# Rotating 96 images by 180 degrees: the last load cut by rows instead of columns, and the first store released by a copy

## The chip, the cores and the metric

The kernel runs on one core of one Trainium2 chip. The metric is the device time of one execution in microseconds (us): 121.89 us is the median of 3 runs before the change (121.85 to 122.08).

## What is computed

The input `x` holds 32 x 3 images of 256 x 256 numbers in float32, 25.17 MB. The reference turns each image by 180 degrees:

```python
def reference(x):
    return np.rot90(x, k=2, axes=(-2, -1)).astype(np.float32)
```

An image read as one line of 65,536 numbers is thus written in reverse order. There is no arithmetic: every byte is read once and written once.

## The kernel before

The 96 images are three groups of 32. In a group, each image is cut into 4 quarters of E = 16,384 numbers (64 KB), which makes 128 rows: row 4n + s is quarter s of image n. A row is one partition of an on-chip tile. The tiles `A`, `Bt` and `Ct` hold the three groups, one each, and all three fit on the chip at once. So a group's work is: load (8.39 MB), reverse each row inside its partition, store.

*Reversal.* `turn` does it in place by the vector engine (DVE), in 4 swaps of J = 2,048 columns from both ends. `swap` makes three copies, all on line 44: the reversed right piece goes to the spare tile `T`, the reversed left piece goes to the right place, and `T` goes to the left place. So a group needs 12 copies. In the profile they are named by tiles: `T<-Bt`, `Bt<-Bt`, `Bt<-T` are the three copies of one swap of group 1. `keep_in_program_order` keeps the copies in the order in which they are written. The order of the four quarters of an image is reversed by the store, which writes quarters with step -1 on the side of the memory (line 50).

*Queues.* Loads and stores are issued by SyncE (SP, the queue `q1`), except the load of `Bt`, which ScalarE issues (queue `q10`). A queue issues in program order, and an instruction whose wait isn't over holds everything behind it on that engine. Behind the queues are 16 DMA engines, which share each transfer by rows; one row, or the part of it that the transfer takes, is one packet. A transfer has a semaphore which is complete when all its rows have landed. A small memset of `Bt` (line 67) precedes the load of `Bt`, and so sets when that load is issued.

*Order.* The loads are issued one after the other at the start: `A`; `Bt` on the other queue; and `Ct` in three transfers (lines 69 to 71):

```python
    rows(2, 0, 0, E)
    ahead = rows(2, 1, 0, E - LAST)
    rows(2, 1, E - LAST, E)
```

They are the 64 even rows; the first 10,624 columns of the 64 odd rows (42,496 B of each row); and their last `LAST` = 5,760 columns (23,040 B of each). Then come the turn of `A`, the store of `A`, the turn and the store of `Bt`, and those of `Ct`.

The store of `A` needs the 12 copies of `A`. A dependence written by hand makes it wait for `ahead` as well, that is, until of all loads only the last columns of the odd rows are under way (lines 80 to 85). The store of `A` is the first on SP after the loads, so the other stores stand behind it.

Of the kernel before, what the change touches and what calls it, by code (L numbers as in the profile page):

```python
# [2 lines left out]

os.environ.setdefault("NEURON_RT_ULTRASERVER_MODE", "4")

# [4 lines left out]


@with_exitstack
def kernel(
    ctx: ExitStack,
    tc: tile.TileContext,
    x: bass.AP,
    out: bass.AP,
):
    nc = tc.nc  # L20
    P = 128

    B, C, H, W = x.shape
    L = H * W
    G = 32
    E = L // 4
    J = E // 8

    x4 = x.rearrange("b c h w -> (b c) (h w)").rearrange(
        "(g n) (s e) -> g (n s) e", n=G, s=4)  # L30
    o4 = out.rearrange("b c h w -> (b c) (h w)").rearrange(
        "(g n) (s e) -> g n s e", n=G, s=4)

    pool = ctx.enter_context(tc.tile_pool(name="slots", bufs=1))
    A = pool.tile([P, E], x.dtype, tag="A")
    Bt = pool.tile([P, E], x.dtype, tag="B")
    Ct = pool.tile([P, E], x.dtype, tag="C")
    T = pool.tile([P, J], x.dtype, tag="T")

    def back(t, lo, hi):  # L40
        return t[:, hi - 1:(lo - 1 if lo else None):-1]

    def copy(dst, src):
        tc.keep_in_program_order(nc.vector.tensor_copy(out=dst, in_=src))  # L44

    def load(t, g, lo, hi, queue=nc.sync):
        return queue.dma_start(out=t[:, lo:hi], in_=x4[g][:, lo:hi])

    def store(t, g, lo, hi):
        return nc.sync.dma_start(  # L50
            out=o4[g][:, ::-1, lo:hi], in_=t[:, lo:hi])

    def swap(t, lo, w):
        hi = E - lo - w
        copy(T[:, 0:w], back(t, hi, hi + w))
        copy(t[:, hi:hi + w], back(t, lo, lo + w))
        copy(t[:, lo:lo + w], T[:, 0:w])

    half = E // 2
    LAST = 5760  # L60

    def rows(g, first, lo, hi):
        return nc.sync.dma_start(
            out=Ct[first::2, lo:hi], in_=x4[g][first::2, lo:hi])

    load(A, 0, 0, E)
    nc.vector.memset(Bt[:, 0:256], 0.0)  # L67
    load(Bt, 1, 0, E, nc.scalar)
    rows(2, 0, 0, E)
    ahead = rows(2, 1, 0, E - LAST)  # L70
    rows(2, 1, E - LAST, E)

    def turn(t, lo, hi):
        while lo < hi:
            w = min(J, hi - lo)
            swap(t, lo, w)
            lo += w

    turn(A, 0, half)
    first = store(A, 0, 0, E)  # L80
    tc.add_manual_dep(
        first.ins, ahead.ins.name,
        mybir.DependencyInfo(
            mybir.DependencyClass.Sync, mybir.DependencyReason.DATA),
        reason="the first store waits for the loads' last columns but a few")
    turn(Bt, 0, half)
    store(Bt, 1, 0, E)
    turn(Ct, 0, half)
    store(Ct, 2, 0, E)


# [1 line left out]
_INS = ['x']  # L93
_OUTS = [((32, 3, 256, 256), 'float32')]


# [23 lines left out]
```

## Time and profile before

| | before |
|---|---|
| median of 3 runs | 121.89 us (121.85 to 122.08) |
| the profiled execution's own time | 122.06 us |
| its span | 120.3 us |
| DVE busy | 44.4 us, 37 instructions |
| a copy of 128 x 2,048 | 1.23 us |
| read and written | 25.17 MB and 25.17 MB, 418 GB/s over the span |
| packets of DMA | 960, 816 of them on q1 |
| first store (`A`) issued | 58.02 us |
| last store (`Ct`) issued | 84.97 us |

The span is the part of the execution from the program's first to its last instruction; the rest lies around it. The page of the profile divides the span into 40 slices of 3 us and shows for each how busy an engine was. An issue's time to landing goes from the instruction that issues the transfer to the completion of its semaphore, so it includes the time in the queue behind earlier transfers. Start times in the timeline are counted from the start of the span.

### The profile page before, as it was taken

To read this page: it belongs to the slowest core of one execution; us is meant where nothing else is said; L and a number is where in the kernel's file an instruction comes from. 1 tells how busy PE (TensorE), PEld (TensorE's weight loads), DVE (VectorE), ACT (ScalarE), POOL (GpSimd) and SP (SyncE) were. 2 spreads that over 40 slices of the span, in tenths; PEclk is the share of its full clock that TensorE was granted. 3 is DMA by queue.
4 is the path that set the end of the run, shared out by engine and by line. 5 is a ranking of instruction groups with operands and counts; after the bars stand their busy time and mean duration, and the time that the engine had idled before them with its cause. 6 is when DMAs were issued, how large, how long until landed. Compare 5 with 4: busy or idle time off the path is not lost.

```text
span 120.3 us, 96 instructions
## 1 busy us (share of the span) xinstructions
DVE 44.4 (37%) x37; POOL 0.2 (0%) x4
## 2 busy tenths in 40 slices
DVE  0000000000000899999999999999200000000000
POOL 0000000000000000000000000000000000000000
DMA  9888988898889988997999889988998899889980
GB/s 349 349 349 371 676 349 349 371 654 371 349 349 654 392 349 349 547 410 327 452 574 480 349 349 545 501 349 349 545 501 349 349 458 589 349 349 436 588 371 0
DMA packets 960, 50.33 MB, mean 418 GB/s; under 512 B 128, under 2 KB 128, under 8 KB 128
## 3 DMA queue, kind: packets, MB, share of 16 engines
q1 hardware_dynamic: 816, 41.94, 81.1%
q10 hardware_dynamic: 144, 8.39, 16.1%
HBM read 25.17 MB, written 25.17 MB: 418 GB/s over the span
## 4 chain that ended last, share of the span: by engine, by line
DVE 37%; DMA 32%; issue 1%
DMA A<-in_x_dram 32%; DVE T L44 12%; DVE A L44 8%; DVE Bt L44 8%; DVE Ct L44 8%
## 5 line engine op out<-in xcount | busy, mean ns | idle before, releaser
L44 DVE COPY T<-A 128x2048 f32<-128x2048 f32 x4 | 4.9, 1226 | 38.6 <-DMA A<-in_x_dram 38.5
L44 DVE COPY A<-A 128x2048 f32<-128x2048 f32 x4 | 4.9, 1227 | 0.1
L44 DVE COPY A<-T 128x2048 f32<-128x2048 f32 x4 | 4.9, 1227 | 0.1
L44 DVE COPY T<-Bt 128x2048 f32<-128x2048 f32 x4 | 4.9, 1227 | 0.1
L44 DVE COPY Bt<-T 128x2048 f32<-128x2048 f32 x4 | 4.9, 1227 | 0.1
L44 DVE COPY T<-Ct 128x2048 f32<-128x2048 f32 x4 | 4.9, 1227 | 0.1
L44 DVE COPY Ct<-T 128x2048 f32<-128x2048 f32 x4 | 4.9, 1227 | 0.1
L44 DVE COPY Bt<-Bt 128x2048 f32<-128x2048 f32 x4 | 4.9, 1226 | 0.1
L44 DVE COPY Ct<-Ct 128x2048 f32<-128x2048 f32 x4 | 4.9, 1226 | 0.1
L67 DVE MEMSET Bt<- 128x256 f32 x1 | 0.3, 272 | 0.9 <-PEq L104 0.9
L104 POOL MEMSET const-bfloat16-1.0<- 128x1 bf16 x1 | 0.1, 101 | 0.0
L104 POOL MEMSET const-uint8-127<- 128x1 uint8 x1 | 0.1, 101 | 0.0
L104 POOL MEMSET const-float32-0.0<- 128x1 f32 x1 | 0.1, 98 | 0.2 <-issue 0.2
L104 POOL MEMSET const-float32-1.0<- 128x1 f32 x1 | 0.1, 98 | 0.0
## 6 DMA issues: line engine op xcount, KB each, us to landing
Ct<-in_x_dram SPq DMA_DIRECT2D x1, 2656.0 KB, 56.2
Ct<-in_x_dram SPq DMA_DIRECT2D x1, 1440.0 KB, 59.1
A<-in_x_dram SPq DMA_DIRECT2D x1, 38.8
Ct<-in_x_dram SPq DMA_DIRECT2D x1, 50.5
Bt<-in_x_dram ACTq DMA_DIRECT2D x1, 43.2
out_dram<-A SPq DMA_DIRECT2D x1, 22.8
out_dram<-Bt SPq DMA_DIRECT2D x1, 30.3
out_dram<-Ct SPq DMA_DIRECT2D x1, 34.5
```

The source lines that it names most:

```text
L44: tc.keep_in_program_order(nc.vector.tensor_copy(out=dst, in_=src))
L67: nc.vector.memset(Bt[:, 0:256], 0.0)
L104: nc = _bacc.Bacc("TRN2", target_bir_lowering=False, num_devices=1)
```

## The change

The odd rows of the third group are no longer cut by columns. They are now two transfers of 32 whole rows each: rows 1, 5, 9, ... and rows 3, 7, 11, .... The sizes of the even rows' load and of all other transfers are the same.

The name `ahead` now stands for the first of these two. The store of `A` no longer waits for it itself. The second copy of the turn of `Bt` (`Bt<-Bt`, called `timer`) does, and the store of `A` waits for the end of that copy. For this, `turn` and `swap` return their copies, and the turn of `Bt` is written ahead of the store of `A`; the order of copies on the DVE stays, and so does the order of transfers on SP.

```diff
     def copy(dst, src):
-        tc.keep_in_program_order(nc.vector.tensor_copy(out=dst, in_=src))
+        c = nc.vector.tensor_copy(out=dst, in_=src)
+        tc.keep_in_program_order(c)
+        return c
+
+    def after(later, earlier, why):
+        tc.add_manual_dep(
+            later.ins, earlier.ins.name,
+            mybir.DependencyInfo(
+                mybir.DependencyClass.Sync, mybir.DependencyReason.DATA),
+            reason=why)
...
-    LAST = 5760
 
-    def rows(g, first, lo, hi):
+    def rows(first, step):
         return nc.sync.dma_start(
-            out=Ct[first::2, lo:hi], in_=x4[g][first::2, lo:hi])
+            out=Ct[first::step, :], in_=x4[2][first::step, :])
...
-    rows(2, 0, 0, E)
-    ahead = rows(2, 1, 0, E - LAST)
-    rows(2, 1, E - LAST, E)
+    rows(0, 2)
+    ahead = rows(1, 4)
+    rows(3, 4)
...
     turn(A, 0, half)
+    timer = turn(Bt, 0, half)[1]
+    after(timer, ahead, "this copy starts when all loads but two rows are in")
     first = store(A, 0, 0, E)
-    tc.add_manual_dep(
-        first.ins, ahead.ins.name,
-        mybir.DependencyInfo(
-            mybir.DependencyClass.Sync, mybir.DependencyReason.DATA),
-        reason="the first store waits for the loads' last columns but a few")
-    turn(Bt, 0, half)
+    after(first, timer, "the first store goes one copy after that")
     store(Bt, 1, 0, E)
     turn(Ct, 0, half)
     store(Ct, 2, 0, E)
```

More of the change, by code (lines that the diff above doesn't have):

```diff
@@ L54, in swap @@
         hi = E - lo - w
-        copy(T[:, 0:w], back(t, hi, hi + w))
-        copy(t[:, hi:hi + w], back(t, lo, lo + w))
-        copy(t[:, lo:lo + w], T[:, 0:w])
+        return [
+            copy(T[:, 0:w], back(t, hi, hi + w)),
+            copy(t[:, hi:hi + w], back(t, lo, lo + w)),
+            copy(t[:, lo:lo + w], T[:, 0:w])]
     half = E // 2
-    LAST = 5760
-    def rows(g, first, lo, hi):
+    def rows(first, step):
         return nc.sync.dma_start(
-            out=Ct[first::2, lo:hi], in_=x4[g][first::2, lo:hi])
+            out=Ct[first::step, :], in_=x4[2][first::step, :])
     load(A, 0, 0, E)
@@ L68 @@
     load(Bt, 1, 0, E, nc.scalar)
-    rows(2, 0, 0, E)
-    ahead = rows(2, 1, 0, E - LAST)
-    rows(2, 1, E - LAST, E)
+    rows(0, 2)
+    ahead = rows(1, 4)
+    rows(3, 4)
     def turn(t, lo, hi):
+        done = []
         while lo < hi:
             w = min(J, hi - lo)
-            swap(t, lo, w)
+            done += swap(t, lo, w)
             lo += w
+        return done
     turn(A, 0, half)
+    timer = turn(Bt, 0, half)[1]
+    after(timer, ahead, "this copy starts when all loads but two rows are in")
     first = store(A, 0, 0, E)
-    tc.add_manual_dep(
-        first.ins, ahead.ins.name,
-        mybir.DependencyInfo(
-            mybir.DependencyClass.Sync, mybir.DependencyReason.DATA),
-        reason="the first store waits for the loads' last columns but a few")
-    turn(Bt, 0, half)
+    after(first, timer, "the first store goes one copy after that")
     store(Bt, 1, 0, E)
```

## The prediction

> **What bounds the kernel now.** I first read the page's slices.
>
> ```profile
> DVE  0000000000000899999999999999200000000000
> DMA  9888988898889988997999889988998899889980
> GB/s 349 349 349 371 676 349 349 371 654 371 349 349 654 392 349 349 547 410 327 452 574 480 349 349 545 501 349 349 545 501 349 349 458 589 349 349 436 588 371 0
> ```
>
> The 16 DMA engines are busy from the first slice to the last but one; the vector engine (DVE) works only in the middle. The 349 and 676 are an artefact: a row is one packet of 64 KB, and its bytes fall into one slice. So I asked for busy time by stretches.
>
> ```profile
> core 0: us, DVE busy (x) POOL busy (x), PEclk, DMA share, GB/s
> 0.00:1.70 1.70, 0.27 (x1) 0.20 (x4) 1.00 0.00 0
> 0.00:2.70 2.70, 0.27 (x1) 0.20 (x4) 1.00 1.13 388
> 5.00:45.00 40.00, 5.29 (x5) 0.00 (x0) 1.00 0.99 431
> 62.00:118.00 56.00, 22.33 (x19) 0.00 (x0) 1.00 0.99 431
> ```
>
> Loads and stores both run at 431 GB/s with the DMA engines 0.99 busy. Nothing moves before 1.70 us, and by 2.70 us 388 GB/s x 2.7 us = 1.05 MB, which is 16 rows of 65,536 B, has started: one row on each engine. Next, the DMA issues with their time to landing, and the timeline and the chain around the switch from loads to stores.
>
> ```profile
> Ct<-in_x_dram SPq DMA_DIRECT2D x1, 2656.0 KB, 56.2
> Ct<-in_x_dram SPq DMA_DIRECT2D x1, 1440.0 KB, 59.1
> A<-in_x_dram SPq DMA_DIRECT2D x1, 38.8
> Ct<-in_x_dram SPq DMA_DIRECT2D x1, 50.5
> Bt<-in_x_dram ACTq DMA_DIRECT2D x1, 43.2
> out_dram<-A SPq DMA_DIRECT2D x1, 22.8
> out_dram<-Bt SPq DMA_DIRECT2D x1, 30.3
> out_dram<-Ct SPq DMA_DIRECT2D x1, 34.5
> ```
>
> ```profile
> 1.14 1.84 SPq L63 DMA_DIRECT2D Ct<-in_x_dram  x3
> ...
> 54.71 1.23 DVE L44 COPY T<-Bt 128x2048 f32<-128x2048 f32 x1
> 55.98 1.23 DVE L44 COPY Bt<-Bt 128x2048 f32<-128x2048 f32 x1
> 57.24 1.23 DVE L44 COPY Bt<-T 128x2048 f32<-128x2048 f32 x1
> 58.02 0.62 SPq L50 DMA_DIRECT2D out_dram<-A  x1
> ```
>
> The three loads of Ct take 562, 596 and 596 ns to issue (that line's own view), so they start at 1.14, about 1.75 and 2.38 us. Adding the times to landing: even rows land at 1.14 + 50.5 = 51.64, the first columns of the odd rows at 1.75 + 56.2 = 57.95, their last columns at 2.38 + 59.1 = 61.48. The stores are issued at 58.02, 69.84 and 84.97 and land at 80.82, 100.14 and 119.47. From the last load on, the landings are 19.34, 19.32 and 19.33 us apart: a full back-to-back chain of DMA. A group has 8 rows on each engine, so a row takes 19.33 / 8 = 2.416 us. 48 rows make 115.97 us; the last landing is at 119.47, so only 3.50 us are not this stream: start-up, the landing of the last row, and whatever is lost in between. The page's chain, which goes through the copies, hides that: the DVE ends its work some 15 us before the last store's turn comes.
>
> **The odd rows.** Before, they are 4 rows on each engine in two cuts (42,496 B and 23,040 B). At 2.416 us a row they should take 9.66 us. They land 61.48 - 51.64 = 9.84 us after the even rows: 0.18 us too much. The first cut accounts for little: 57.95 - 51.64 = 6.31 against 9.66 x 42,496 / 65,536 = 6.27. The other 0.14 us is lost in the last columns (3.53 against 3.40), the piece beside which the first store is issued. After, each engine has 2 + 2 whole rows, so 8 packets become 4. If the loss comes from the cuts, all 0.18 us go. If it comes from issuing a store beside loads, up to 0.14 us stay. The nearest rows on issuing beside whole rows: the second and third store are issued in the middle of other stores, and those intervals (19.32, 19.33) show no loss; but these are not loads. I take half, **-0.09 us**, and keep -0.18 and 0 as the ends.
>
> **The new release.** Two of four odd rows are in at 51.64 + 2 x 2.416 = 56.47 us, 1.48 us before the old first cut (57.95). The timer is the second copy of B's turn, Bt<-Bt. Before, it starts at 55.98; now it waits for 56.47 and, with 0.07 us from landing to start as the old store had (57.95 to 58.02), starts at 56.54. It ends 1.24 us later at 57.78, and the store goes at about **57.80** (the step from the last copy of B, ending at 69.82, to its store, at 69.84, is 0.02). That is 0.22 us earlier than before. The last odd rows land at 51.64 + 9.66 = 61.30, with the old 0.04 to 0.18 on top if the loss stays. So from issue to the last load's landing there are at least 61.30 - 57.80 = 3.50 us, against 61.48 - 58.02 = 3.46 before, and before no time was lost between the last load and the first store (19.34, like the others). So the lead is still enough: cost **0** for the switch. The cover is not thin: the load of A, issued at 0.73, had a row on every engine by 2.70, that is within 1.97 us from an empty queue. The trace's packets show that the first engine went from loads to stores at 60.35 and the last at 61.11, without a gap, so 60.35 - 58.02 = 2.33 us from issue were enough. Now there are about 2.5 (60.3 - 57.80), and 57.80 + 1.97 = 59.77 is 0.5 us ahead of the first engine's need. Without that cover, each microsecond of delay would be one of the kernel's time.
>
> **What stands behind the wait.** On the DVE, the timer holds 22 later copies: 10 of B and 12 of Ct, each moved by 56.54 - 55.98 = 0.56 us. B's store is then issued at 70.40, while the first store still fills the engines until about 80; Ct's at 85.53, needed at about 99. Slack 9 us and more: cost 0. On SP, the first store holds the other two stores, which wait for copies much later anyway. The old direct wait of the store on the load is gone; it waits for the copy alone, beside A's load. No instruction is added: the same three loads on SP and the same 36 copies, and the same semaphore per load.
>
> **The issue at the start.** The two last loads of Ct now have 32 rows rather than 64, and are issued beside the first rows in flight. The rows do not show an issue time that goes by rows: 128 rows of A took 0.36 us, 64 rows 0.56 to 0.60. So I take 0; bounds: nothing, or half of 2 x 0.60 us, if it did go by rows and all of it delayed the stream.
>
> **The sum.** Profiled execution: 122.06 us, of which the span is 120.3 and 1.76 lie outside it. 122.06 - 0.09 + 0 + 0 = 121.97. The profiled execution is the upper one of a group whose runs are 121.85, 121.89 and 122.08; the median 121.89 may hold less of the loss, so I take -0.07 off the median: **121.82**. With the ends 0 and -0.18, this case spans 121.71 to 121.89. That is inside 0.2% (0.24 us), about what a measurement of this kernel can tell from no change.
>
> [...] What no row shows is a pitch of four rows (256 KB) between the rows of a load; A is read with 64 KB pitch and Ct with 128 KB, the latter at full speed (Bt landed at 44.36, the even rows 7.28 us later, three rows of 2.416 being 7.25). [...]
>
> **Rivals.** *Faster, by the start* (chance 0.27): half-size loads make the issue stretch 1.14 to 2.98 shorter and the first rows, which start by 2.70, run freer. Of the 3.50 us outside the stream, 0.73 come before the first issue and 1.97 until all engines have started, which leaves 0.8 for slow first rows, landing and the odd rows' 0.18. The gain would be 0.18 plus 0.1 to 0.4, at most 0.6: say -0.4, **121.5**. Against it: issue time not going by rows.
>
> *Slower, by a late first store* (0.23): the store's descriptors reach the engines after they have run dry, because its release now hangs on a copy. Place: the SP queue at 57.80. It decides from about 60.3 - 1.97 = 58.33 on, so a slip of over 0.5 us; a slip by one copy (1.26 us) leaves the engines idle for 0.7 us. With the part of the 0.18 that comes off, +0.3 to +0.7: **122.3** at the middle to low end. For it: a copy that is a timer adds every delay of the DVE's wait to the store's path. Against: all steps above have rows, and the sum has half a microsecond left.
>
> *32 rows not spread over all 16 engines* is a part of the slower side, at most 0.02: on 8 engines, the odd rows would take 19.33 us and not 9.66, +9.7. All transfers of the trace, of 128 and of 64 rows, show all engines busy.
>
> **Chances and range.** Forecast case 0.50; faster 0.27; slower 0.23. The range goes from 121.45 to 122.30: it takes in the forecast's 121.71 to 121.89, some two thirds of the faster and half of the slower case, and leaves out about 0.2. The forecast case's own range is 121.71 to 121.89.
>
> **What would show it.** The copy Bt<-Bt at about 56.5 instead of 55.98, waiting for Ct's load by about 0.5 us; the first store at 57.8; landing of the loads about 56.5 and 61.3 to 61.5; stores again 19.33 apart, the first one too; B's and Ct's stores issued 0.5 us later with no effect. Wrong, if the first store lands more than 19.5 us after the last load (late release), if the loads of A land clearly before 39.55 (start), or if an odd row takes other than 2.42 us.

## The result: 0.19% slower

The changed kernel takes 122.25 us (median of 22 runs, 121.81 to 122.64); the kernel before, run beside it, 121.99 us (22 runs, 121.81 to 122.44). The ratio is 1.0019, interval 1.0011 to 1.0027: about 0.23 us slower. The forecast was 121.82 us, a small gain. The time lies inside the stated range of 121.45 to 122.30, but on the other side of no change, and outside the forecast case's own 121.71 to 121.89. The fastest run of each is the same, 121.81 us: what the change adds is a loss that some runs have more of than others. The profiled execution of the changed kernel is the slowest of its group (122.64 us, span 120.9), so its trace shows the loss large.

First the DMA issues of the changed kernel, as they are on its page, then those of the three loads of Ct by themselves (duration of the issue in ns, start, and time to landing: least, median, most).

```profile
Ct<-in_x_dram SPq DMA_DIRECT2D x3, 54.7
...
out_dram<-A SPq DMA_DIRECT2D x1, 23.6
out_dram<-Bt SPq DMA_DIRECT2D x1, 30.3
```

```profile
L72 SPq DMA_DIRECT2D Ct<-in_x_dram x3: 573/593/687, 1.2 to 2.5; - x3
...
DMA to landing us min/median/max: 50.5/54.7/59.6
```

And its timeline around the release of the first store:

```profile
54.67 1.23 DVE L44 COPY T<-Bt 128x2048 f32<-128x2048 f32 x1
56.59 1.23 DVE L44 COPY Bt<-Bt 128x2048 f32<-128x2048 f32 x1 [0.69 <-DMA Ct<-in_x_dram]
57.84 0.62 SPq L59 DMA_DIRECT2D out_dram<-A  x1
```

The loads of Ct are issued at 1.15, 1.77 and 2.50 us and land at 51.63, 56.49 and 62.09. The first 32 odd rows take 56.49 - 51.63 = 4.86 us; two rows of 2.416 us make 4.83. The last 32 take 62.09 - 56.49 = **5.60 us**, 0.77 too much. The first store lands at 81.42, 19.33 us after the last load, so nothing is lost between them. From the even rows on, the loads take 10.46 us instead of 9.66: a loss of 0.80 us, against 0.18 in the kernel before. The 0.62 us between these two losses are the difference between the two profiled executions (122.64 - 122.06 = 0.58), to within 0.04.

The trace's packets show where it sits: on every one of the 16 engines, the fourth odd row, the last before the engine's first store, takes 0.14 to 0.71 us longer than 2.42 (0.33 on the mean). The third, and all rows of the stores, take 2.42; the second takes 0.04 more on the mean. The late release can be struck out at once: no engine waits between its last row and its first store (in order of time, the steps are 0.003 us at most).

### The profile page after: what moved, and what is told of

Its sections match the earlier page's. It is cut to its first block, busy times and chain, and to the rows that moved or that the text cites. A ratio compares the mean times of both kernels' runs of the same rounds, so it can differ in the third digit from the quotient of the medians.

```text
span 120.9 us, 97 instructions
## 1 busy us (share of the span) xinstructions
DVE 44.4 (37%) x37; POOL 0.2 (0%) x4
## 4 chain that ended last, share of the span: by engine, by line
DVE 37%; DMA 32%; issue 1%; another core or an unknown queue 0%; DVEq 0%
DMA A<-in_x_dram 32%; DVE T L44 12%; DVE Bt L44 8%; DVE A L44 8%; DVE Ct L44 8%; DVEq L44 0%
```

## The experiments

Two numbers are worked out for each run from its profile, in the same way. **Loss** is the landing of the last load, less the landing of the even rows, less 9.66 us. A transfer lands with its slowest engine (in the changed kernel the 16 engines end the last load between 61.14 and 62.09 us, and it lands at 62.09), so this goes by the slowest of the 16. **Lead** is how far ahead of the undisturbed end of the loads the first store is issued: landing of the even rows, plus 9.66, less the issue. For the kernel before: 51.64 + 9.66 - 58.02 = 3.28 us; for the changed one 51.63 + 9.66 - 57.84 = 3.45.

### Is it the issue of the store beside the loads?

The changed kernel, with the first store held until all loads are in (e1):

```diff
-    ahead = rows(1, 4)
-    rows(3, 4)
+    rows(1, 4)
+    ahead = rows(3, 4)
...
-    timer = turn(Bt, 0, half)[1]
-    after(timer, ahead, ...)
+    turn(Bt, 0, half)
...
-    after(first, timer, ...)
+    after(first, ahead, "the first store waits for all loads")
```

> After's whole rows, but the first store waits for the landing of all loads (no timer). Measure: from the landing of the first 32 odd rows to that of the last 32, 4.83 us if nothing is lost; after the change it was 5.60. Theory 'issue' (issuing the store beside a row in flight slows that row): with no store issued beside loads the interval is 4.83 to 4.90 and the last load lands at about 61.35; the store is issued at about 61.4 and the engines then idle for 1.5 to 2 us, so the run is 1.0 to 1.5 us longer than after. Theory 'rows' (the last 32 rows are slow by themselves, by their pitch or place): the interval stays at 5.3 to 5.6. Theory 'late store' (the prediction's slower rival) has no time here: it would show only in the gap between last load and first store.

The loads' own view, and the SP queue:

```profile
L72 SPq DMA_DIRECT2D Ct<-in_x_dram x3: 562/594/599, 1.2 to 2.4; - x3
...
DMA to landing us min/median/max: 50.5/54.7/59.0
```

```profile
69.87 0.63 SPq L59 DMA_DIRECT2D out_dram<-Bt  x1
70.60 0.57 SPq L59 DMA_DIRECT2D out_dram<-A  x1
```

The most that a load takes is 59.0 instead of 59.6. With 51.66, 56.50 and 61.40 us for the landings, the last 32 rows take 4.90 us, and the loss by the rule above is 0.08: figures under 0.1 mean no loss. So the same whole rows with the same pitch are not slow by themselves; the loss needs the store. The time (132.37 us, ratio 1.0848) says nothing more, and missed what was expected of it: the store of Bt came to stand ahead of that of A in the queue, so no store went before 69.87 us and the engines stood for 10 us.

### Small pieces, and other rows

Five kernels keep the timer and its release on the landing of half of the odd rows.

e2, odd rows in two halves by columns (`rows` takes columns again, as in the kernel before):

```diff
-    rows(0, 2)
-    ahead = rows(1, 4)
-    rows(3, 4)
+    rows(0, 0, E)
+    ahead = rows(1, 0, half)
+    rows(1, half, E)
```

> After's timer and release, but the odd rows cut by columns into two halves (64 x 32,768 B each), so that the same bytes are under way at the same time in pieces of half the size. First half lands at about 56.5, store issued at about 57.8 as after. Theory 'cut' (a whole row in flight is what suffers, small pieces suffer less): the second half takes 4.85 to 5.1 us instead of 5.60, and the time is within 0.1% of before. Theory 'issue by itself': the loss depends on the time of the issue only, the second half takes 5.4 to 5.7 and the time is 0.1 to 0.3% over before, as after.

Measured: ratio 0.9995 (0.9984 to 1.0006); the halves land at 56.66 and 61.61, the second takes 4.95; lead 3.40, loss 0.19. At this point theory "cut" stood as expected, though the store went at 58.01, 0.17 us later than in the changed kernel.

e3 and e4, odd rows one by one, in the order 5, 7, 1, 3 or 1, 3, 5, 7 of each eight (the edit of e3 is shown):

```diff
-    ahead = rows(1, 4)
-    rows(3, 4)
+    rows(5, 8)
+    ahead = rows(7, 8)
+    rows(1, 8)
+    rows(3, 8)
```

> After's timer, but the odd rows go as four transfers of 16 rows, one row on each engine, in the order 5, 7, 1, 3 of each eight rows; the timer waits for the second, so the store is issued at the same time (about 57.8), while row 3 of each eight is in flight rather than row 7. In both traces the slowed packets were the third and fourth of a Ct transfer (before) or rows 5 and 7 (after), never rows 0 to 3 of eight. Theory 'place' (rows 4 to 7 of each eight are the sensitive ones): the last two rows take 4.83 to 5.0 us and the time is 0.1 to 0.3% under after; rows 5 and 7 lose little, since no store is issued beside them. Theory 'issue': whichever row is in flight is slowed, 5.3 to 5.7 us, time as after.

> The control of the run before: the same four transfers of 16 rows in the order 1, 3, 5, 7, the timer on the second. Row 7 of each eight is in flight when the store is issued. Both 'issue' and 'place' expect what after showed: 5.3 to 5.7 us for the last two rows, 0.1 to 0.3% over before. If it loses nothing, the size of the transfers (32 rows against 16) has to do with it.

Both missed, and test nothing of what they were made for. They take 132.53 and 132.58 us (ratios 1.0864 and 1.0866). The five loads of Ct in the first:

```profile
L72 SPq DMA_DIRECT2D Ct<-in_x_dram x5: 582/589/620, 1.2 to 3.7; - x5
...
DMA to landing us min/median/max: 51.3/59.9/68.5
```

The four transfers of 16 rows land about 5 us apart (52.41, 57.56, 62.38, 67.53, 72.20), though each has one row for each engine. In the packets, all 16 engines are at work, but a row takes 4.4 to 5.1 us and not 2.42: about half the rate. Rows in steps of 4 run at 2.43 us a row (4.86 / 2). Why is not shown: against a step of 4, a step of 8 puts the rows eight partitions apart on the chip and not four, 512 KB apart in the memory and not 256 KB, and halves the rows of a transfer, and no run changes one of these without the others.

e8, the last rows alone in halves:

```diff
     ahead = rows(1, 4)
-    rows(3, 4)
+    for lo in (0, half):          # rows 3, 7, ..., half the columns
+        nc.sync.dma_start(
+            out=Ct[3::4, lo:lo + half], in_=x4[2][3::4, lo:lo + half])
```

> After, but the last 32 odd rows go as two halves by columns (2 x 32 x 32,768 B; one transfer more); the first 32 whole, timer and store at 57.8 as after. Theory 'cut' (it is the whole row in flight beside the issue that suffers): the last rows take 4.85 to 5.05 us, as with all odd rows cut in halves (4.95), and the time is 0 to 0.1% off before. If instead the pitch of four rows is what matters, they take 5.3 to 5.7 although they are cut.

Ratio 1.0004 (0.9993 to 1.0014), but the last rows take 61.67 - 56.42 = 5.25 us; lead 3.46, loss 0.44. Small pieces, and more loss than "cut" allows (5.05 at most), though a little less than the 5.3 expected of the pitch. The time fits "cut".

e5, the changed kernel again:

> The changed kernel itself once more, for a second profile. If the loss in the last 32 odd rows belongs to the kernel, they take 5.2 to 5.8 us again (5.60 in the first profile, 4.83 undisturbed, 4.95 with half-row pieces) and nearly every engine's last row is stretched; the time is 0.1 to 0.3% over before. If the first profile caught an accident, they take 4.85 to 5.0.

Ratio 1.0009 (1.0000 to 1.0019). The last 32 rows take 61.52 - 56.42 = 5.10; lead 3.47, loss 0.28. Between the two expected cases: with the same lead, the loss differs from execution to execution by half a microsecond.

### The time of the release

The store without the timer, waiting directly for the first 32 odd rows (e6), and the store one copy later (e7):

```diff
-    timer = turn(Bt, 0, half)[1]
-    after(timer, ahead, ...)
+    turn(Bt, 0, half)
...
-    after(first, timer, ...)
+    after(first, ahead, ...)
```

> After's whole rows without the timer: the first store waits directly for the first 32 odd rows, so it is issued at about 56.6 instead of 57.84, some 3.7 us before the loads' end, and its issue is over by about 57.3, before the last row of any engine starts (58.2). Theory 'issue beside a whole row' (the row in flight at the issue, and about 1 us after it, is slowed): the loss moves to the third odd row and the last row is partly spared; the total from the even rows' landing to the last one stays 10.0 to 10.5 us (9.66 undisturbed). Theory 'last row before the store' (what is slowed is the row that is followed by a store in the queue, whenever that was issued): the last row is stretched as after, 5.3 to 5.8 us for the last 32 rows. If an early issue is harmless, 4.85 to 5.0, and the time is 0.1 to 0.3% below after.

```diff
-    timer = turn(Bt, 0, half)[1]
-    after(timer, ahead, ...)
+    timer = turn(Bt, 0, half)[1:3]
+    after(timer[0], ahead, ...)
...
-    after(first, timer, ...)
+    after(first, timer[1], "the first store goes two copies after that")
```

> After with the store one copy later: the timer is followed by one more copy, and the store is issued at about 59.1, some 1.2 us before the first engine runs out of loads. Theory 'issue beside a whole row': the row in flight is the same one, already a third done, and is still slowed by 0.2 to 0.7 us; or the descriptors come just after the row's end, then the last 32 rows take 4.85 to 5.0 but the engines wait up to 0.7 us between last load and first store. Either way 0.1 to 0.6% over before. If both are small, the later release is the better one: time at or under before.

The SP queue's issue of the first store in e6, its loads, and the issue in e7:

```profile
56.55 0.62 SPq L59 DMA_DIRECT2D out_dram<-A  x1
```

```profile
L72 SPq DMA_DIRECT2D Ct<-in_x_dram x3: 566/593/622, 1.2 to 2.4; - x3
...
DMA to landing us min/median/max: 50.5/54.7/59.8
```

```profile
59.15 0.63 SPq L59 DMA_DIRECT2D out_dram<-A  x1
```

In e6 the store is issued 1.3 us earlier than in the changed kernel, and the kernel takes 122.92 us: ratio 1.0083 (1.0071 to 1.0095). Lead 4.74, loss 0.98. In the packets the third odd row, in flight at the issue, is untouched (2.42), and the fourth takes 1.0 us longer on the mean. So "issue beside a whole row" falls, and "last row before the store" holds. One copy later (issue at 59.15, lead 2.21) the loss is 0.02, but the ratio is 1.0015 (1.0006 to 1.0023): the early loss is gone and a late one begins. The packets of this execution show it. Over the 16 engines the gap between the last load and the first store is 0.04 us on the mean, and the rows of the stores take 2.42 to 2.47 us (at most 2.43 in the changed kernel), which over the 24 store rows of an engine adds up to 0.19 us on the mean. So the last store lands 119.45 - 61.38 = 58.07 us after the last load, against 120.04 - 62.09 = 57.95 in the changed kernel. Why these rows are longer is open. (The 0.47 us that a later expectation names for one engine rests on a pairing of packets with engines that the trace does not give; in order of time, no engine's gap is over 0.11 us.)

### Does it grow with the lead, and do small pieces help?

The whole rows with no wait at all (f1), the kernel before with no wait (f2), and the same with last columns of 1,024 (f3):

```diff
 # changed kernel
-    after(timer, ahead, ...)
-    after(first, timer, ...)
```

> After's whole rows, and the first store waits for nothing but the copies of A: issued at about 54.8, when three of four odd rows are still to come on some engines. Measured so far: issue at 57.8, last row of an engine stretched by 0.33 and 0.17 us on the mean of 16 engines; issue at 56.55, by about 0.97; issue at 59.15, by 0. Only the last row was stretched each time. Theory 'last piece' (the piece that has a store behind it in its engine's queue is stretched, for as long as the store is there, whichever time it was issued): the last row alone is stretched again by 0.9 to 1.1 us, the third not at all, and the time is that of the issue at 56.55 (0.7 to 0.9% over before). Theory 'issue in flight': the second odd row (53 to 56) is stretched, the last one not. If the stretch grows with the lead, it is over 1.5 us.

```diff
 # kernel before
-    tc.add_manual_dep(first.ins, ahead.ins.name, ...)
```

> The kernel before without the wait of the first store (issued at about 54.8); the odd rows end in pieces of 23,040 B (0.855 us). Theory 'last piece': only the last piece is stretched, and in proportion to its size, 0.3 to 0.5 us on the mean of the engines, time 0.2 to 0.3% over before. Theory 'read ahead by bytes' (what is stretched is the last 64 KB or so of loads, in however many pieces): 0.9 to 1.1 us over the last three pieces, time 0.7 to 0.9% over before.

```diff
 # kernel before
-    LAST = 5760
+    LAST = 1024
...
-    tc.add_manual_dep(first.ins, ahead.ins.name, ...)
```

> The same without the wait, and with last pieces of 1,024 columns (4,096 B, about 0.15 us each). Theory 'last piece': the stretch falls to under 0.1 us, the last load lands 9.7 to 9.8 us after the even rows, and the time is 0 to 0.15% under before: no timing of the release is needed. Theory 'read ahead by bytes': the pieces of 61,440 B ahead of it are stretched, and the loss is 0.5 us or more.

The release and the loads of f1:

```profile
54.78 0.62 SPq L59 DMA_DIRECT2D out_dram<-A  x1
```

```profile
L72 SPq DMA_DIRECT2D Ct<-in_x_dram x3: 566/594/644, 1.2 to 2.5; - x3
...
DMA to landing us min/median/max: 50.5/54.8/60.1
```

| | lead, us | loss, us | ratio to before |
|---|---|---|---|
| f1, whole rows, no wait | 6.58 | 1.23 | 1.0088 (1.0069 to 1.0106) |
| f2, columns of before, no wait | 6.60 | 1.13 | 1.0084 (1.0065 to 1.0102) |
| f3, last columns 1,024, no wait | 6.59 | 1.14 | 1.0079 (1.0066 to 1.0091) |

"Last piece" falls: whatever the cut, about 1.1 to 1.2 us are lost. With pieces of 4,096 B at the end, the row pieces of 61,440 B ahead of them are stretched (2.9 to 3.4 us each, where the earlier ones take 2.27). With those of 23,040 B, the last three of an engine's four take 0.13, 0.70 and 0.16 us longer on the mean. So it is the last 64 KB or so of an engine's loads that is slowed while a store stands behind it in the queue, in however many packets. That is what "read ahead by bytes" expected; the cause in its name is the author's guess and was not shown.

### Lead or whole rows

A short pause on the DVE (a memset of a spare tile of 256 columns in g1, 512 in g2) between the timer and the store shortens the lead of the whole rows:

```diff
+    D = pool.tile([P, 256], x.dtype, tag="D")
...
+        if t is Bt and lo == 0:       # in swap, between its second and third copy
+            pauses.append(nc.vector.memset(D[:], 0.0))
+            tc.keep_in_program_order(pauses[0])
...
-    after(first, timer, ...)
+    after(first, pauses[0], "the first store goes a short pause after that")
```

> After, with a pause of 0.27 us (a memset of a spare tile of 256 columns) between the timer and the store: issue at about 58.1, lead 3.18 us. Lead means here: the landing of the even rows plus 9.66 us (the undisturbed end of loads) less the issue of the first store. Leads and losses so far: before 3.28, loss 0.18; after 3.45 and 3.47, loss 0.80 and 0.28; issue at 56.55 lead 4.74, 0.98; no wait 6.6, 1.1 to 1.2 whatever the cut; two copies 2.21, 0.02. Theory 'lead' (only the lead decides, on a steep part between 3 and 4.7 us): loss 0.05 to 0.2, time within 0.1% of before, 0.1% or more under after. Theory 'whole row' (at these leads a whole row suffers more than cut pieces): loss 0.2 to 0.6, time still 0.05 to 0.2% over before.

> The same with a pause of about 0.53 us: issue at about 58.35, lead 2.9 us. Theory 'lead': loss 0 to 0.1, time 0 to 0.15% under before unless engines run dry (with lead 2.21, one of 16 engines did for 0.47 us). Theory 'whole row': loss 0.1 to 0.3, time as before or 0.1% over.

and a larger last cut (g3) lengthens that of the kernel before; in g4 the pause is also tried with columns in halves (the edit of e2 and the one above together):

```diff
 # kernel before
-    LAST = 5760
+    LAST = 6912
```

> The kernel before with the odd rows cut earlier (last columns 6,912 instead of 5,760): the first cut lands 0.68 us earlier, so the store is issued at about 57.35, lead 3.96 us, with pieces of 27,648 B at the end. Theory 'lead': a loss between those of 3.46 and 4.74 us, 0.4 to 0.8 us, time 0.2 to 0.5% over before though the rows are cut. Theory 'whole row': the small pieces keep the loss at 0.15 to 0.3, time within 0.1% of before.

> Odd rows as two halves by columns, the timer, and a pause of 0.27 us: lead about 3.18 with pieces of 32,768 B. If both lead and pieces count, this is the best of all: loss 0 to 0.15, time 0 to 0.15% under before. If only the lead counts, the same time as the whole rows with the same pause.

The DVE and the SP queue with the short pause, and the DMA issues with the larger last cut:

```profile
57.76 0.27 DVE L71 MEMSET D<- 128x256 f32 x1
57.95 1.17 DVE L45 COPY Bt<-T 128x2048 f32<-128x2048 f32 x1
58.06 0.63 SPq L60 DMA_DIRECT2D out_dram<-A  x1
```

```profile
Ct<-in_x_dram SPq DMA_DIRECT2D x1, 2368.0 KB, 55.5
Ct<-in_x_dram SPq DMA_DIRECT2D x1, 1728.0 KB, 59.9
```

In the first, the store goes at 58.06 instead of 57.84. In the second the rows are cut, and yet the last load takes 59.9 us to land, where before it took 59.1. The last three runs, h1 to h3, complete a square: cut or whole rows, at the lead of before or of the changed kernel.

```diff
 # h1: kernel before
-    LAST = 5760
+    LAST = 6048
 # h2: the changed kernel as it is
 # h3: the changed kernel with a pause of 128 columns
```

> The kernel before with last columns of 6,048 instead of 5,760: pieces of 24,192 B, and the store issued 0.17 us earlier, at a lead of about 3.46 us, that of after. With before itself (cut, lead 3.29), the next run (whole rows, 3.46) and the last (whole rows, 3.29) this is a square of four. Theory 'lead alone': 0.1 to 0.2% over before, like after. Theory 'whole rows too': under 0.08% over before.

> The changed kernel a third time, on the same chip as the run before (whole rows, lead 3.46): 0.08 to 0.2% over before by both theories.

> The changed kernel with a pause of about 0.17 us (memset of 128 columns): whole rows at a lead of about 3.29 us, that of before. Theory 'lead alone': within 0.06% of before. Theory 'whole rows too': 0.05 to 0.15% over before.

The release in h1 and in h3:

```profile
57.73 0.62 SPq L50 DMA_DIRECT2D out_dram<-A  x1
```

```profile
58.12 0.62 SPq L60 DMA_DIRECT2D out_dram<-A  x1
```

| | odd rows | lead, us | loss in the profile, us | ratio to before |
|---|---|---|---|---|
| e7, two copies | whole | 2.21 | 0.02 | 1.0015 (1.0006 to 1.0023) |
| g2, long pause | whole | 2.95 | 0.01 | 1.0000 (0.9992 to 1.0009) |
| g1, short pause | whole | 3.19 | 0.41 | 0.9997 (0.9986 to 1.0009) |
| g4, short pause | halves | 3.19 | 0.09 | 0.9993 (0.9984 to 1.0001) |
| before | cut | 3.28 | 0.18 | 1 |
| h3, pause of 128 | whole | 3.34 | 0.05 | 0.9999 (0.9990 to 1.0008) |
| e2, timer | halves | 3.40 | 0.19 | 0.9995 (0.9984 to 1.0006) |
| h1, LAST = 6,048 | cut | 3.46 | 0.40 | 1.0010 (1.0000 to 1.0020) |
| e8, timer | last rows in halves | 3.46 | 0.44 | 1.0004 (0.9993 to 1.0014) |
| changed, first time | whole | 3.45 | 0.80 | 1.0019 (1.0011 to 1.0027) |
| changed, e5 | whole | 3.47 | 0.28 | 1.0009 (1.0000 to 1.0019) |
| changed, h2 | whole | 3.49 | 0.49 | 1.0009 (0.9998 to 1.0020) |
| g3, LAST = 6,912 | cut | 3.95 | 1.04 | 1.0053 (1.0035 to 1.0072) |
| e6, no timer | whole | 4.74 | 0.98 | 1.0083 (1.0071 to 1.0095) |

Within the noise of about 0.1%, the time goes by the lead: a flat floor from about 2.9 to 3.4 us, a steep part above, and a rise at 2.2. Whole rows at the lead of before cost nothing (h3, 0.9999), nor do they at shorter leads (g1, g2). Cut rows at longer leads cost what whole rows do, as far as these intervals tell: h1 1.0010 against 1.0009 to 1.0019 at 3.46, and g3 1.0053 between the whole rows at 3.46 and 4.74. The theory "lead" met its expectations in g2, h2 and h3, and in h1 at their lower edge; in g3 the way was right and the loss (1.04 for 0.4 to 0.8) and the time (0.53% for 0.2 to 0.5) came out over it. In g1 the time was as expected, and the loss of that one profile (0.41 for 0.05 to 0.2) was not; there a single row of the last 16 is stretched, by 0.33 us, and the others by 0.01 at most. "Whole row" fell in g3, by time and loss; in g1 and h3 the times lie below what it expected, though their intervals do not exclude its 0.05%, and the loss of g1 fits it. g4 fits both of its cases. What speaks against a pure account by lead: the halves at 3.40 (0.9995) and the cut last rows at 3.46 (1.0004) are a little better than the line, by no more than their intervals and the scatter between executions. A small share for the cut is not excluded. No version beats the kernel before clearly; the best is the halves with a pause, 0.9993 (0.9984 to 1.0001).

## Why the prediction was wrong

**What held.** The bound was right: the engines are busy from the loads to the end (0.99 of the time from 62 to 118 us in the changed kernel), and the stores stay 19.33 us apart. The release was right step by step: the first 32 odd rows were expected at 56.47 and landed at 56.49; the timer at 56.54 and 56.59; the store at 57.80 and 57.84; B's and Ct's stores at 70.40 and 85.53, and 70.45 and 85.58. The 22 delayed copies cost nothing.

**What failed is the term for the odd rows.** It was -0.09 us with ends -0.18 and 0, on the ground that the loss of 0.18 us could stay or go. It could also grow, and did: 0.80, 0.28 and 0.49 in three profiles, so that odd rows took other than 2.42 us, one of the prediction's own signs of being wrong. The two causes that the step weighed were the cuts and the issue of a store beside loads. The cuts were not it, or a small share at most (whole rows at the lead of before: 0.9999). The other was near, but the rule was missing: what counts is not that a store is issued there but how far ahead of the loads' end it is issued (a loss of 0.02 us at a lead of 2.21, of 0.98 at 4.74), and what loses is the last 64 KB of an engine's loads (1.0 us longer on the mean in e6). The rows it leaned on, the second and third store issued beside other stores without loss, were no neighbours of this case: there a store follows stores. Nor do loads queued behind loads lose anything like it (431 GB/s from 5 to 45 us in the kernel before, as for its stores).

**The lead was compared with the wrong end.** The step on the release set 61.30 - 57.80 = 3.50 us beside 61.48 - 58.02 = 3.46 and called the lead as before. But 61.48 held the loss itself. Against the undisturbed 61.30, the lead of before was 3.28, and the change lengthened it to 3.45, by 0.17 us. The step asked only whether the store might come too late, and set the price of coming earlier at 0. An estimate from h1 and g3: from 3.46 to 3.95 us, 0.43% or 0.5 us of time go with 0.5 us of lead, and at that slope 0.17 us of lead would be worth about 0.17 us. The 22 runs show 0.23, the two repeats 0.11 each.

**The rivals.** The late first store fell: no engine waited in the changed kernel, and 0.44 us more of delay costs nothing (g2, 1.0000). The slower side had the right sign with the wrong mechanism, and it is luck that the range, drawn up to 122.30 for a late store, takes in a loss from an early one. A late edge there is, another copy on (e7, 1.0015). The faster start fell: the three issues of Ct take 1.94 us, not less than the 1.84 before, and A's first copy starts at 39.54 against 39.58. The spread of 32 rows over 16 engines held: 2.43 us a row. The row pitch cost nothing in this change: at 256 KB, the undisturbed rows take 4.86 us for two against 4.83.

## What to carry to other kernels

When the last loads and the first stores share a saturated queue, as here (431 GB/s, the DMA engines 0.99 busy), price an early side of the store's release as well as a late one: in these runs up to 1.2 us are lost when it is queued long ahead, 0.1 to 0.2% when it is 0.2 us too early, and nothing that a noise of 0.1% lets see between 2.9 and 3.3 us ahead of the loads' end. At 2.2 us it is late, and 0.15% are lost again. When a release is moved, work out its lead against the undisturbed end of what is ahead of it, both before and after, and price both signs. A small loss that the profile shows at such a place may be the foot of a steep slope, so it is no upper bound.

## What the runs showed of the hardware

With a store queued behind them well ahead (leads of 4.74 and 6.58 us, e6 and f1), the last 64 KB of an engine's loads took 0.7 to 1.4 us longer (3.12 to 3.85 us for a row of 2.42), nearly the same whether that store was issued 1.4 or 3.2 us before the first such row began (1.0 and 1.2 us on the mean). When it was issued 0.3 us before (57.84, the row at 58.18), they took 0.14 to 0.71 us longer. The load rows ahead of them in e6 and f1, and the stores behind stores in the changed kernel, took 2.42 to 2.43. With the store at a lead of 2.21 us (e7), the rows of the stores took up to 2.47 us. Why is open for both. Transfers of 16 rows, eight partitions and 512 KB apart, ran at about half the rate (e3: 5 us a row) on all 16 engines; 32 rows, four partitions and 256 KB apart, at the full rate (2.43 us a row in the changed kernel). That difference is unexplained, too.
